# A second pair of solve tiles, and more dense work per recurrence step, in a two-layer hybrid backbone

## The chip, the cores and the metric

The kernel runs on one NeuronCore of a Trainium2 chip. The metric is the device time of one execution in microseconds (us). Each time given for the kernel is a median over runs; the rows come from one further execution that was profiled.

## What is computed

The reference is a backbone of two layers over 1024 latent tokens (x) and 256 context tokens (c) of width 1024. Cut to what matters here, a layer does this, in float32:

```python
ux = modulate(rmsnorm(h)) @ w_in          # 17 blocks of 128 columns
y_rwkv, y_rwkv_c = rwkv7(ux, uc)          # recurrence, forwards and backwards,
                                          # context first, then the latent tokens
y = concat(y_rwkv, pool(ux), fourier(ux), conv(ux))
h  = h + gt1 * (y @ w_out)
h  = h + gt2 * ((silu(g) * u) @ ffn_w_out)     # g, u = modulate(rmsnorm(h)) @ ffn_w_in
hc = the same for the context                  # in layer 0 only
```

The context tokens never read the latent ones, and after layer 0 only the inputs of the context's recurrence are needed. So the whole output side of the context (projection `w_out`, feed-forward) exists in layer 0 alone.

## The kernel before, in words

**Engines and precision.** Every dense product is made of three TensorE matmuls per 128-row piece of the weights: weights and activations are each split into a rounded high part (ACT, a copy, line 324) and the remainder (a subtraction on DVE or POOL, line 325). A 256 KB piece of weights is 128x512 values: one load issued by SP, one ACT copy, one subtraction, twelve matmuls.

**The order of the work.** The program is written as generators that a hand-made weave (`_Weave`) advances; the framework then assigns tiles and orders each engine's instructions by the position in the program and a simulated timeline, so an engine's order is fixed before the run. Within an engine, and on SP's queue of transfers, instructions start in that order.

**The recurrence** (`rwkv2`, line 800) works in chunks: ten stages per layer, two of the context and eight of x, each holding 128 tokens of both directions. An iteration `it` runs from -3 to 9, has 14 gaps (`GAPS`), and carries several stages at once:

- `prep` of stage it+3, from gap 8 (line 896): decays and scaled keys; ACT, POOL lines 921, 943, 957, 971, DVE lines 926 (a scan), 947 to 956.
- `inner` of stage it+2, from gap 0 into the next iteration (line 973): products of keys masked by DVE (line 991) into W; 32x32 blocks of it go through a DRAM tensor `Ad` (line 995) and come back laid out as 32 small triangular systems per partition group in two tiles `As0`, `As1` (line 1001); POOL sets their diagonals (line 1029); then the **solve** (lines 1031 to 1052), a chain of small DVE operations in eight blocks, four from each tile; its result leaves through `Td` (line 1056) and comes back (line 1062).
- `front_b` of stage it+1 (line 1069): merges the solved halves, and transposes values.
- `chain` of stage it (line 1133): the state itself, two chunks with three or four small matmul groups and ACT copies each.
- `finish` of stage it-1 (line 1192): group norm, bonus and gate; for a context stage its end sets `R.ctx`.

The tiles of the recurrence are rings (`rg`, line 855) cut out of one pool `t2` of 73 tiles of 128x512 values. Counted from the code, the rings, the mask and the four tiles of small weights hold 69 of them at most; `As0` and `As1` are one tile each.

**Dense work in the recurrence.** In each gap `W.fill(cost)` draws that many microseconds of dense work (by the program's own count, 1/2.4 ns per matmul column) from the generator `fill` (line 1324). How much is drawn per gap is `FILL[layer]`, by iteration: up to -2, -1, and from 0 on. In layer 0 the generator gives, in order: the remaining input projections; the Fourier mixer (`four2`); then nothing until the convolution and pooling are through and the context's recurrence is read out (`R.ctx`, set late in iteration 2); the output projection of the context and of both halves of x (`outp`, line 1648); the context's second norm (`norm2c`); and the first feed-forward product of the context for `NC` of its 22 blocks (`ffn1_ctx`, line 1621). What is left when the recurrence ends is drawn in the stage behind it (the share of the output projection that reads the recurrence's own output, residuals, x's second norm), and the rest flushed at its end (line 1497). During the recurrence the subtraction of line 325 is on POOL.

**The feed-forward of x** (`ffn1`, line 1541) runs 22 blocks of seven products each. For blocks from `NC` on, it also computes the context's block with the same weights, on four more groups of matmuls (lines 1577 to 1617) and one more split (line 1533).

Of the kernel before, what the change touches and what calls it, by code (L numbers as in the profile page):

```python
# [22 lines left out]
NFF = 22  # L23
# [20 lines left out]
MODPE = ((2, 1), (3, 0), (4, 1))  # L44
MK = 7
FR = "c2"
FILL = ((2.6, 1.2, 0.9), (2.3, 1.0, 0.9))
LA = 2
NC = 14
ORD = (1, 0)  # L50
OFILL = (1.0, 0.3, 0.8, 1.0)
LOP = (0, 2, 4)
# [40 lines left out]
class _Kernel:  # L93
# [706 lines left out]
    def rwkv2(s, R, fill):  # L800
# [7 lines left out]
        for it in range(-3, N):  # L808
# [9 lines left out]
            for g in range(GAPS):  # L818
# [23 lines left out]
                W.step()  # L842
                W.fill(FILL[R.l][min(max(it + 2, 0), 2)])
            for _ in ch:
# [6 lines left out]
        while W.live:  # L851
            W.step()
            W.fill(FILL[R.l][2])

# [118 lines left out]
    def inner(s, R, F):  # L973
# [21 lines left out]
                    nc.sync.dma_start(Ad[b, d, :, h].rearrange("u j i -> j u i"), W[r0:r0 + 32, :, 32 * b:32 * b + 32])  # L995
            yield

        As = [s.rg(R, f"As{a}", 1) for a in range(2)]
        Adf = Ad.rearrange("b d u h j i -> (b d u h) (j i)")
        for a in range(2):  # L1000
            nc.sync.dma_start(As[a], Adf[:, a * 512:(a + 1) * 512].unsqueeze(0).broadcast_to([4, 32, 512]))
# [254 lines left out]
    def run(s, nlayers):  # L1256
# [43 lines left out]
        for l in range(nlayers):  # L1300
# [23 lines left out]
            def fill():  # L1324
# [10 lines left out]
                if not last:  # L1335
                    yield from norm2c()
                    for f in range(NC):
                        yield from s.ffn1_ctx(l, f, [a[2] for a in acts2], hid[f])

            def norm2c():  # L1340

                for _ in range(2):
                    yield
                s.lab("norm2")
                hc = s.rows(NK, ("c",))
                for k in range(NK):
                    h2[k][2] = hc[k][2]
                    nc.sync.dma_start(hc[k][2], ho[k][:, 1024:1280])
                yield
                r = yield from s.rstd_g([h2[k][2] for k in range(NK)], 256, D, 0, False, "ps", lambda j: s.t2())  # L1350
                for k in range(NK):
                    acts2[k][2] = s.act_row(("c",))[2]
                for _ in s.norm_g(l, 1, h2, 2, acts2, r):
                    if _ % 2:
                        yield
# [145 lines left out]
    def ffn1_weights(s, l, ctx):  # L1501
# [11 lines left out]
        def sp(x):  # L1513
            hi, lo = s.t2(F32R, "f2"), s.t2(F32R, "f2")
            nc.scalar.copy(hi, x)  # L1515
            s.nw += 1
            (nc.gpsimd if s.nw % 7 in LOP else nc.vector).tensor_tensor(lo, x, hi.bitcast(F32), ALU.subtract)  # L1517
            return hi, lo
# [3 lines left out]
        for f in range(NFF):  # L1522
# [9 lines left out]
            yield sp(a12)  # L1532
            if ctx and f >= NC:
                yield sp(a21)
# [6 lines left out]
    def ffn1(s, l, wg, acts, B, bc, hid):  # L1541
# [4 lines left out]
        def take():  # L1546
            while len(q) <= LA:
                w = next(wg, None)
                if w is None:
                    break  # L1550
                q.append(w)
            return q.pop(0)
# [15 lines left out]
        for f in range(NFF):  # L1568
            s.lab("ffn")
            ctx = bc[0] is not None and f >= NC  # L1570
            w = take()
# [320 lines left out]
```

## Time and profile before

| what | us |
|---|---|
| median of 3 runs | 3343.46 (3340.38 to 3346.46) |
| the profiled execution | 3351.38 |
| its span, first to last instruction | 3349.6 |
| PE busy | 3000.7 (90%) |
| DVE, POOL, ACT busy | 2109.8, 1385.8, 1257.5 |
| mean granted TensorE clock | 0.911 |

The span is read by stages. Layer 0's recurrence reaches to 910, the stage behind it to about 1104, its feed-forward's first product to 1541, the second to about 1820; layer 1 repeats the order, with its recurrence ending at 2594. "PE busy" counts time with a matmul in flight, whatever the clock; the granted clock of a stretch is a share of full speed (1.0 is 2.4 GHz, 0.5 is 1.2 GHz), so the two together say how much of a stretch TensorE could still take. The chain of waits follows the execution back from its last instruction, each time to what released it.

### The profile page before, as it was taken

The numbers are of one execution on the slowest core, as the hardware profiler recorded it, in microseconds if no ns is written. First come the engines' busy times: TensorE is split into PE (matmuls) and PEld (weight loads), VectorE is DVE, ScalarE is ACT, GpSimd is POOL, SyncE is SP. The second block draws the span as 40 slices with busy tenths as digits, with TensorE's granted clock in tenths as the row PEclk, the third lists the DMA queues.
The fourth block names the chain that finished last, engine by engine and source line by source line (L and its number), as shares of the span: only waits on it lengthen the run. The fifth ranks groups of instructions, "written<-read, shape, count | busy, mean of one in ns | idle before, by whom it ended". The sixth has DMA issues, their size and how long they took to land.

```text
span 3349.6 us, 52386 instructions
## 1 busy us (share of the span) xinstructions
PE 3000.7 (90%) x18888; PEld 2410.5 (72%) x18888; DVE 2109.8 (63%) x3498; ACT 1257.5 (38%) x2575; POOL 1385.8 (41%) x1484
## 2 busy tenths in 40 slices
PE   6989997877889999999999978988877799999998
PEld 3657765766678888888888766756665588888787
DVE  6679666666374988644545598666665755554535
ACT  4446433443363222223212455333443433333212
POOL 2366224563168554435310064245550454545400
PEclk8989887787899999999999988987787799999999
DMA  7422344465455444337412212345553322224312
GB/s 265 165 92 97 102 117 136 124 174 156 144 190 164 149 132 151 125 98 233 139 35 78 87 53 90 117 134 139 156 159 88 128 92 79 82 89 164 123 39 78
DMA packets 375818, 415.48 MB, mean 124 GB/s; under 512 B 115587, under 2 KB 214916, under 8 KB 375558
## 3 DMA queue, kind: packets, MB, share of 16 engines
q1 hardware_dynamic: 375558, 412.13, 39.4%
q8 instruction: 149, 2.44, 0.3%
q14 instruction: 111, 0.91, 0.1%
HBM read 306.49 MB, written 100.27 MB: 121 GB/s over the span
## 4 chain that ended last, share of the span: by engine, by line
PE 55%; DVE 14%; DMA 9%; issue 3%; SPq 1%; ACT 1%; POOL 1%; DVEq 0%; POOLq 0%; ACTq 0%
PE pc L153 17%; PE ps L153 17%; PE pb L153 14%; PE pf L153 8%; DMA t<-Ad 3%; DVE c L532 2%; DMA Td<-t 1%; DVE t L1050 1%; DVE t L947 1%; DVE t L1043 1%; DVE f L325 1%; DVE t L956 1%; DVE t L1469 1%; DMA t<-ho 1%; DVE t L1493 1%
## 5 line engine op out<-in xcount | busy, mean ns | idle before, releaser
L153 PE MATMUL pc<-t,f 128*128 128x512 f32 (+1 forms) x3108 | 754.4, 392 | 41.3 <-ACT t L427 16.0
L153 PEld LDWEIGHTS pc<-t,f 128*128 128x128 f32 x3108 | 581.6, 195 | 182.9 <-ACT t L427 20.5
L153 PE MATMUL ps<-t,f 128*128 128x512 f32 (+1 forms) x2094 | 517.0, 393 | 18.4 <-ACT t L324 7.7
L153 PE MATMUL pb<-t,f 128*128 128x512 f32 (+1 forms) x2094 | 470.5, 370 | 8.4 <-ACT t L1468 4.9
L153 PEld LDWEIGHTS ps<-t,f 128*128 128x128 f32 x2094 | 390.8, 190 | 99.8 <-ACT t L324 8.2
L153 PEld LDWEIGHTS pb<-t,f 128*128 128x128 f32 x2094 | 370.4, 190 | 78.8 <-ACT t L1468 6.0
L1515 ACT CAST f<-c 128x512 fp32r<-128x512 f32 x316 | 196.0, 621 | 536.7 <-PE ps L153 132.0
L1517 POOL TENSOR_TENSOR f<-c,f 128x512 fp32r<-128x512 f32 x135 | 186.5, 1381 | 426.2 <-ACT f L1515 411.7
L153 PE MATMUL pf<-t,f 128*128 128x512 f32 (+2 forms) x1500 | 314.2, 364 | 14.2 <-DVE t L1044 4.0
L324 ACT CAST f<-m 128x512 fp32r<-128x512 f32 (+1 forms) x236 | 134.7, 576 | 436.3 <-PE pb L153 226.4
L153 PEld LDWEIGHTS pf<-t,f 128*128 128x128 f32 (+1 forms) x1500 | 249.5, 198 | 61.4 <-ACT f L324 4.4
L530 POOL TENSOR_TENSOR c<-c,cp 128x352 f32<-128x352 f32 (+2 forms) x168 | 183.3, 1092 | 145.9 <-ACT c L523 71.3
L1517 DVE TENSOR_TENSOR f<-c,f 128x512 fp32r<-128x512 f32 x181 | 158.6, 878 | 134.8 <-ACT f L1515 134.4
L153 PE MATMUL pf<-c,f 128*128 128x512 f32 (+1 forms) x704 | 200.5, 416 | 30.0 <-DVE t L1684 20.3
L325 POOL TENSOR_TENSOR t<-c,t 128x512 fp32r<-128x512 f32 (+1 forms) x110 | 135.1, 1266 | 173.8 <-PE ps L153 99.5
L153 PE MATMUL ps<-t,t 64*128 64x128 f32 (+2 forms) x1032 | 159.9, 341 | 38.9 <-DVE t L956 23.4
L532 DVE SCALAR_TENSOR_TENSOR c<-c,dv,c 128x352 f32<-128x352 f32 (+2 forms) x238 | 190.5, 829 | 2.0
L153 PEld LDWEIGHTS ps<-t,t 64*128 64x128 f32 (+1 forms) x1032 | 133.6, 231 | 60.4 <-issue 20.4
L153 PEld LDWEIGHTS pc<-t,t 128*64 128x64 f32 (+2 forms) x2484 | 124.6, 161 | 71.8 <-issue 28.6
L153 PE MATMUL pc<-t,t 128*64 128x64 f32 (+3 forms) x2484 | 156.2, 258 | 20.9 <-DMA t<-t 11.8
L153 PEld LDWEIGHTS pf<-c,f 128*128 128x128 f32 x704 | 131.5, 214 | 60.1 <-issue 19.1
L261 DVE SCALAR_TENSOR_TENSOR cp<-m,sc,cp 128x512 f32<-128x512 f32 x140 | 137.5, 1003 | 43.0 <-DMA m<-in_wmod 42.3
(256 smaller groups left out, 4731.3 us busy)
## 6 DMA issues: line engine op xcount, KB each, us to landing
c<-in_ffin SPq DMA_DIRECT2D x176, 256.0 KB
m<-in_wmod SPq DMA_DIRECT2D x116, 256.0 KB
t<-rw SPq DMA_DIRECT2D x232, 128.0 KB
hid<-t SPq DMA_DIRECT2D x88, 256.0 KB
c<-hid SPq DMA_DIRECT2D x88, 256.0 KB
m<-in_ffout SPq DMA_DIRECT2D x80, 256.0 KB
t<-in_wmod SPq DMA_DIRECT2D x76, 256.0 KB
m<-in_win SPq DMA_DIRECT2D x64, 256.0 KB
```

Source lines behind the costliest of these rows:

```text
L153: s.nc.tensor.matmul(o, l, r, start=start, stop=stop)
L261: nc.vector.scalar_tensor_tensor(acc[t], w, sc, acc[t], ALU.mult, ALU.add)
L324: r = s.nc.scalar.copy(hi, src)
L325: (eng or s.lo_eng).tensor_tensor(lo, src, hi.bitcast(F32), ALU.subtract)
L530: nc.gpsimd.tensor_tensor(g, g, t_, ALU.add)
L532: nc.vector.scalar_tensor_tensor(a, w[:, j:j + m], tap(j), a, ALU.mult, ALU.add)
L947: nc.vector.scalar_tensor_tensor(KRv[:, :, p, 0, 1:64], k2[:, :, p, 1:64], -2.0, P2[:, :, p, 0:63], ALU.mult, ALU.mult)
L956: nc.vector.tensor_tensor(BKv[rows, :, :, 1 - h, :], cv(kd)[rows], cv(iP)[rows], ALU.mult)
L1043: nc.vector.tensor_tensor(tv, at(x, o, [0, m], [1, 4], [32, 4]), at(T_, r0, [32, m], [0, 4], [1, 4]), ALU.mult)
L1050: nc.vector.tensor_tensor(tv, at(x, o + 4, [0, m], [1, n], [32, 4]), at(T_, r0, [32, m], [0, n], [1, 4]), ALU.mult)
L1515: nc.scalar.copy(hi, x)
L1517: (nc.gpsimd if s.nw % 7 in LOP else nc.vector).tensor_tensor(lo, x, hi.bitcast(F32), ALU.subtract)
```

## The change

`FILL` of layer 0 draws 1.5 instead of 1.2 per gap in iteration -1, and 1.6 instead of 0.9 from iteration 0 on; layer 1 keeps its values. `NC` becomes 22 (`NFF`), so that all of the context's blocks come from `ffn1_ctx`, and `ffn1` computes none (the condition `f >= NC` of lines 1533 and 1570 never holds). `As0` and `As1` get two tiles each, in both layers.

```diff
-FILL = ((2.6, 1.2, 0.9), (2.3, 1.0, 0.9))
+FILL = ((2.6, 1.5, 1.6), (2.3, 1.0, 0.9))
 LA = 2
-NC = 14
+NC = NFF
...
-        As = [s.rg(R, f"As{a}", 1) for a in range(2)]
+        As = [s.rg(R, f"As{a}", 2) for a in range(2)]
```

## Rows read from the trace of the kernel before

**Rows 1.** The page's head.
```profile
span 3349.6 us, 52386 instructions
```

**Rows 2.** Busy time by stretch: PE, PEld, DVE, ACT, POOL, clock, DMA share, GB/s.
```profile
716.00:764.00 48.00, 39.30 (x381) 29.86 (x381) 31.57 (x64) 20.18 (x55) 31.14 (x46) 0.89 0.68 192
845.00:882.00 37.00, 37.00 (x350) 27.10 (x350) 15.39 (x24) 13.93 (x34) 11.90 (x13) 1.00 0.48 146
627.00:910.00 283.00, 236.05 (x2395) 186.87 (x2393) 165.02 (x358) 110.45 (x285) 125.73 (x187) 0.83 0.54 152
910.00:1064.00 154.00, 132.97 (x990) 117.81 (x991) 90.53 (x108) 85.53 (x158) 104.86 (x74) 0.93 0.53 174
...
1341.00:1541.00 200.00, 200.00 (x1080) 173.73 (x1078) 111.08 (x153) 56.80 (x98) 77.58 (x55) 1.00 0.36 116
...
2482.00:2527.00 45.00, 32.90 (x372) 26.58 (x370) 32.30 (x71) 16.86 (x48) 17.74 (x31) 0.73 0.49 147
...
2594.00:2664.00 70.00, 47.42 (x280) 36.18 (x281) 49.64 (x64) 33.30 (x61) 23.03 (x15) 0.78 0.45 154
```

**Rows 3.** Single lines: count, min/median/max ns, first and last start in us.
```profile
L1684 DVE SCALAR_TENSOR_TENSOR t<-pf,mod,t x24: 471/737/751, 630.1 to 898.8; 128x512 f32<-128x512 f32 x16, 128x256 f32<-128x256 f32 x8
...
L1246 DVE TENSOR_TENSOR t<-t,pb x5: 674/686/690, 606.9 to 909.7; 128x512 f32<-128x512 f32 x5
...
L1638 DVE TENSOR_TENSOR cp<-pf,cp x14: 407/420/425, 958.7 to 1075.2; 128x256 f32<-128x256 f32 x14
...
L1576 ACT COPY t<-pc x4: 579/582/582, 1103.9 to 1282.8; 128x512 f32<-128x512 f32 x4
...
L1576 ACT COPY t<-pc x3: 577/586/586, 1342.2 to 1493.2; 128x512 f32<-128x512 f32 x3
...
L1576 ACT COPY t<-pb x7: 580/581/582, 2684.3 to 3026.6; 128x512 f32<-128x512 f32 x7
```

**Rows 4.** Groups by line, 1030 to 1075: busy us, mean ns, idle before.
```profile
L153 PE MATMUL pf<-t,c 128*128 128x256 f32 x356 | 43.4, 284 | 0.2 <-POOL c L325 0.2
...
L325 POOL TENSOR_TENSOR c<-m,c 128x512 fp32r<-128x512 f32 x26 | 33.0, 1293 | 8.8 <-ACT c L324 8.7
L324 ACT CAST c<-m 128x512 fp32r<-128x512 f32 x25 | 15.4, 619 | 20.6 <-DMA m<-in_ffin 16.4 <-PE pf L153 3.5 <-POOL c L325 0.4
```

**Rows 5.** Who waited at line 1029 (us, times), and the chain of waits, 620 to 760.
```profile
  DMA t<-Ad: 173.3, 33
...
638.18 1.22 DVE t L926
...
665.30 0.69 DVE t L991
...
669.99 10.09 DMA t<-Ad
...
680.13 0.13 POOL t L1029
```

**Rows 6.** Timeline of SP's queue: start, us, line, transfer.
```profile
664.67 2.12 SPq L995 DMA_DIRECT2D Ad<-t  x4
...
668.25 0.57 SPq L1001 DMA_DIRECT2D t<-Ad  x1
...
669.99 4.68 SPq L1001 DMA_DIRECT2D t<-Ad  x1
```

**Rows 7.** Timelines of POOL and DVE, one solve operation twice.
```profile
667.28 1.28 POOL L325 TENSOR_TENSOR f<-m,f 128x512 fp32r<-128x512 f32 x1 [6.21 <-ACT f L324]
...
667.54 1.06 DVE L1052 TENSOR_TENSOR t<-t,g 128x28 f32<-128x28 f32 x1
...
676.99 0.20 DVE L1052 TENSOR_TENSOR t<-t,g 128x28 f32<-128x28 f32 x1
```

**Rows 8.** Timelines of ACT and PE: a late weight.
```profile
680.54 0.62 ACT L324 CAST f<-m 128x512 fp32r<-128x512 f32 x1 [7.31 <-DMA m<-in_wout]
...
681.21 0.80 PE L153 MATMUL pf<-c,f 128*128 128x256 f32 x2 [5.14 <-ACT f L324]
```

## The prediction

> **What bounds the kernel now.** I read the busy table by stretch first, multiplying PE's busy time by the granted clock of its row: that is the work at full speed, and the rest of the stretch is lost to idling or to the half-speed clock. Three kinds of stretch appear [rows 2].
>
> - Layer 0's recurrence, from the first output projection (630) to the last read-out (910) [rows 3]: 283 us, 236.0 busy at 0.83 = 196 us of work, 87 lost. No engine is full; it runs on latencies.
> - The stage behind it, 910 to 1064: 132.97 x 0.93 = 124 of work, 30 lost. All 14 context blocks run here (958.7 to 1075.2) [rows 3]. I end it at 1064 because the third block of x's feed-forward copies at 1103.9, and a block takes (1282.8 - 1103.9) / 9 = 19.9 [rows 3].
> - The feed-forward with the context in it, 1341 to 1541: PE 200.00 of 200.00 at clock 1.00. TensorE is the bound, and only fewer matmuls help.
>
> The chain of waits says what the recurrence's latency is. POOL's diagonal for one solve ends at 638; the next stage's scan starts at once (638.18), its masked products come at 665.30, the load of its triangles at 669.99 takes 10.09, and POOL's next diagonal is at 680.13 [rows 5]: a loop of some 42 us, closed because POOL runs this diagonal ahead of the next stage's `prep`.
>
> **The change part by part.**
>
> *Eight context blocks leave x's feed-forward.* With the context a block takes (1493.2 - 1342.2) / 6 = 25.2, without it 19.9 [rows 3]. Eight times 5.3 is 42 us, on a full TensorE: gone from there.
>
> *They reappear in the dense generator.* A block there has 48 matmuls of 256 columns at 43.4 / 356 = 0.122 us, so 5.85 us [rows 4]; eight are 47 us of PE. Each also brings four loads of 256 KB, four ACT copies (0.62) and four POOL subtractions (1.29) [rows 4]; eight splits of the old path go. That is 32 loads more in all.
>
> *The generator is drawn faster.* From the read-out of the context to the end of iteration 9 there are seven iterations. By the program's own count they drew 7 x 12.6 = 88, of which the output projection takes 82 (20.5 for the context, 30.7 for each half of x): the recurrence ended with the blocks still to do. Now they draw 7 x 22.4 = 157, and the read-out behind them some 19: about 18 of 22 blocks move into the recurrence, the rest stays behind it. Iterations 0 to 2 gain nothing, as the generator gives nothing until `R.ctx`.
>
> *What it costs there.* Total PE work from 627 to the start of x's feed-forward becomes 196 + 124 + 47 = 367. The question is what is lost beside it. For steps with a solve I compare two: 24 us of work in 45 (2482 to 2527) and 35 in 48 (716 to 764) [rows 2]: 11 more work, 3 more time. A step of the new kernel has some 46; on that slope it takes about 51 and loses about 5 or 6. Four such steps lose 24; iterations 7 to 9 and the read-out, with few solves left, I put at 12 together, since 845 to 882 is already full (37.00 of 37.00, clock 1.00) [rows 2]. Bounds: 0 lost, or 87 as now. I take 36, nearer to the full step, because most of the blocks fall into such steps. Behind the recurrence the nearest row is layer 1's same stage, with no dense work left: 70 us, 47.42 x 0.78 = 37 work, 33 lost [rows 2]; three or four blocks fill some: 26.
>
> So 367 + 36 + 26 = 429 instead of 437 (627 to 1064), 8 less, and with the 42 about 50 us.
>
> *Queues.* Eighteen moved blocks put 18 x 5 transfers on SP at up to 0.57 us each [rows 6], 51 us over some 330; SP's issues have room, but a load that waits for a free buffer holds up the triangles behind it. ACT (110 of 283 busy) and DVE (165) [rows 2] have room. POOL takes 18 x 4 x 1.29 = 93 us more on 126 [rows 2, 4]; the loss of 5 or 6 per step stands for this queueing, and the second rival prices it in full.
>
> *The second pair of tiles.* It removes a wait of the triangles' load for the solve before. On SP the products are written at 664.67, the first load goes at 668.25, the second, which waits for the solve, at 669.99 [rows 6]: 1.7 us later, 1.1 more than the 0.57 of an issue. The load is late because its data are. So about 1 us per step: 6 in layer 1, 3 in layer 0 before the dense steps take over, 9 in all. From above: POOL's waits for these loads sum to 173 us over both layers [rows 5], some 85 per layer; if the scheduler moved them off the loop, layer 1 would gain up to 70. From below: two of the four tiles that the pool had free are gone, and a reordered POOL could block longer: 20 us lost.
>
> **A rule against it.** One solve operation of 28 elements takes 1.06 us beside a POOL subtraction of 1.28 and 0.20 alone [rows 7], so 0.86 of delay can ride on each moved subtraction. The Trainium skill ("SBUF — State Buffer", "SBUF: two separate sides") says why: GpSimd and a VectorE operation with two SBUF inputs exclude each other for the whole instruction. By that rule, with every moved subtraction hitting the solve, the sum would lose 18 x 4 x 0.86 = 62 more and the gain would be gone. I take it as part of the 36, since most blocks come when the last solve is done; the slower rival uses the delay.
>
> **The sum.** 50 + 9 = 59 off the profiled 3351.4 (a span of 3349.6 [rows 1] and 1.8 around it) is 3292. The median of the runs stands 7.9 below the profile, so I forecast 3285. A measurement can tell about 0.2%, 6.7 us.
>
> **The rivals.**
>
> 1. *Forecast:* dense work fills the idling, TensorE nearly full; 3250 to 3315. Chance 0.56.
> 2. *The triangles' load leaves the loop as well.* The scheduler, free of the old wait, puts POOL's diagonal elsewhere, and layer 1 gains its 70. For it: 173 us of waits [rows 5]. Against: the products come 4 us before the load is issued, so there is nothing to load earlier. 3285 - 64 = 3221. Chance 0.13.
> 3. *Slower: POOL, in the loop, becomes the bound.* Between one diagonal and the next load stand `prep`'s POOL operations, and weight subtractions between them. The context's projection puts 8 more into its step (10 us), x's projection 2.5 blocks more per step (a full and a half subtraction each, 1.94: 4.8, three times), the first step with context blocks 18 of 1.29 less the 6 us there now (16): 41 us on the loop if none hides. A late weight stops PE as well (5.14 us behind a copy that waited 7.31 [rows 8]), and the chain behind it in PE's order. Then the recurrence loses 87 + 41 = 128, not 36: 3285 + 92 = 3377. It decides against the change once the loss passes 95, that is, once the dense work adds to the steps in full and the idling stays. Against: the slope of 3 us for 11. Chance 0.18.
> 4. *The blocks don't fit in.* The context's norm needs 12 tiles of a pool with 2 to 4 free until `prep` of the last stage is through in iteration 6 or 7. If all 22 blocks then run behind the recurrence, 47 are added there and 42 taken from x's feed-forward; with the 9, 3340. Chance 0.13.
>
> **How the numbers follow.** Faster by over 0.2%: 0.56 + 0.13 and a little of case 4, 0.71; within: 0.11; slower: 0.18. The range takes in case 2 and case 4 and leaves out case 3 and a stronger case 2: 3217 to 3350. The forecast's own is 3250 to 3315.
>
> **What would show it.** Right: the context's blocks mostly between 770 and 960; the recurrence's read-out later, near 960 instead of 910, with clock above 0.9; the stage behind it some 75 us; every block of x's feed-forward at 19.9; layer 1's recurrence unchanged within 10 us. Wrong: context blocks still behind the read-out (case 4); layer 1's loop well below 42 us (case 2); the read-out past 1020, POOL full and PE's clock no higher (case 3).

## The result and the profile after

The changed kernel takes 3370.38 us (median of 4 runs, 3362.7 to 3373.65) beside 3341.92 for the kernel before on the same chip (4 runs, 3336.74 to 3346.46): 1.0082 times, 95% interval 1.0059 to 1.0105, 28 us slower where 57 faster was forecast. Its profiled execution is the fastest of its four (3362.70), and that of before stood above its median, so the two profiles differ by 11 us only; stage by stage they are compared as they are.

Single lines of the kernel after, as in [rows 3] (count, min/median/max ns, first and last start in us):

```profile
L1684 DVE SCALAR_TENSOR_TENSOR t<-pf,mod,t x24: 467/742/751, 656.2 to 882.1; 128x512 f32<-128x512 f32 x16, 128x256 f32<-128x256 f32 x8
...
L1246 DVE TENSOR_TENSOR t<-t,pb x5: 672/676/687, 621.3 to 971.9; 128x512 f32<-128x512 f32 x5
...
L1638 DVE TENSOR_TENSOR cp<-pf,cp x8: 423/424/426, 908.0 to 965.8; 128x256 f32<-128x256 f32 x8
...
L1638 DVE TENSOR_TENSOR cp<-pf,cp x22: 409/423/426, 908.0 to 1119.9; 128x256 f32<-128x256 f32 x22
...
L1576 ACT COPY t<-pb x8: 579/581/589, 1081.9 to 1523.2; 128x512 f32<-128x512 f32 x8
...
L1612 DVE TENSOR_TENSOR t<-t,t x22: 675/871/1716, 1096.5 to 1540.4; 128x512 f32<-128x512 f32 x22
```

The last of these rows (line 1612 follows the last of x's seven products in each block) in the kernel before:

```profile
L1612 DVE TENSOR_TENSOR t<-t,t x22: 677/694/1074, 1032.1 to 1540.4; 128x512 f32<-128x512 f32 x22
```

The output projection begins 26 us later than before (656.2 against 630.1 [rows 3]), the recurrence is read out 62 later (971.9 against 909.7), and 8 of the 22 context blocks are done by then (the third row), 14 behind it. x's feed-forward starts its last block at 1523.2; before, that row read 1519.0, but there the last block still had the context in it, some 5 us more to do: line 1612 starts for the last time at 1540.4 in both. So layer 0 has gained nothing: all that its feed-forward saved had been spent.

Busy time by stretch, kernel after (columns as in [rows 2]): the recurrence from the begin of the output projection to the read-out, the stage behind, the feed-forward, and layer 1's recurrence.

```profile
656.00:972.00 316.00, 268.56 (x2806) 216.77 (x2807) 180.89 (x362) 140.85 (x336) 174.42 (x214) 0.91 0.59 165
972.00:1107.00 135.00, 121.47 (x851) 107.90 (x849) 86.01 (x94) 76.35 (x136) 94.39 (x66) 0.92 0.54 181
1186.00:1506.00 320.00, 320.00 (x1464) 266.62 (x1463) 252.59 (x328) 97.00 (x163) 163.80 (x114) 1.00 0.44 142
2084.00:2614.00 530.00, 426.63 (x3801) 323.60 (x3800) 335.58 (x735) 199.50 (x507) 207.69 (x360) 0.79 0.46 126
```

Two of these for the kernel before, on its own marks:

```profile
630.00:910.00 280.00, 233.05 (x2363) 184.27 (x2362) 165.02 (x358) 109.69 (x283) 123.91 (x184) 0.83 0.54 153
...
2085.00:2594.00 509.00, 419.78 (x3797) 314.84 (x3795) 328.68 (x736) 198.32 (x506) 208.09 (x359) 0.82 0.47 131
```

Work is busy time times clock again. From the output projection's begin to the read-out it is 268.56 x 0.91 = 244 us in 316, where before it was 233.05 x 0.83 = 193 in 280: 51 more work cost 36 more time. In the feed-forward TensorE is full (320.00 of 320.00 at clock 1.00), and every block takes the 20 us of one without the context. Layer 1, where the second pair is the only edit, takes 530 us from its first scan to its last read-out instead of 509.

POOL's wait at line 1029 for the triangles, which the second pair was to shorten, grew from 173.3 us [rows 5]:

```profile
  DMA t<-Ad: 222.1, 35
```

With the pair alone it is 185.3, with the faster draw of iterations -1 to 2 alone 190.7.

### The profile page after: what moved, and what is told of

Read it like the earlier page. It is cut to its first block, busy times and chain, and to the rows that moved or that the text cites. A ratio compares the mean times of both kernels' runs of the same rounds, so it can differ in the third digit from the quotient of the medians.

```text
span 3360.9 us, 52525 instructions
## 1 busy us (share of the span) xinstructions
PE 2989.7 (89%) x18888; PEld 2400.5 (71%) x18888; DVE 2127.6 (63%) x3487; ACT 1277.9 (38%) x2605; POOL 1440.3 (43%) x1519
## 4 chain that ended last, share of the span: by engine, by line
PE 58%; DVE 20%; DMA 11%; issue 4%; POOL 3%; SPq 2%; ACT 2%; DVEq 0%; POOLq 0%; ACTq 0%
PE ps L153 17%; PE pc L153 17%; PE pb L153 14%; PE pf L153 10%; DVE c L532 4%; DMA t<-Ad 3%; DVE t L1050 1%; DMA Td<-t 1%; DVE t L1043 1%; DVE t L956 1%; DMA t<-in_wmod 1%; DVE t L1493 1%; DVE t L1052 1%; DVE t L947 1%; DVE t L401 1%
## 5 line engine op out<-in xcount | busy, mean ns | idle before, releaser
L1517 POOL TENSOR_TENSOR f<-c,f 128x512 fp32r<-128x512 f32 x132 | 179.7, 1361 | 418.8 <-ACT f L1515 397.7
L153 PE MATMUL pf<-t,f 128*128 128x512 f32 (+2 forms) x1116 | 260.7, 389 | 15.8 <-DMA f<-eo 4.7
L153 PEld LDWEIGHTS pf<-t,f 128*128 128x128 f32 (+1 forms) x1116 | 199.2, 199 | 60.9 <-ACT t L427 5.2
L153 PEld LDWEIGHTS pc<-t,t 128*64 128x64 f32 (+2 forms) x2484 | 117.7, 153 | 68.0 <-issue 38.6
L153 PE MATMUL pc<-t,t 128*64 128x64 f32 (+3 forms) x2484 | 147.5, 250 | 18.6 <-DMA t<-t 13.7
```

What stands on the lines that cost most here:

```text
L153: s.nc.tensor.matmul(o, l, r, start=start, stop=stop)
```

## The experiments

Each was run beside the kernel before, in five groups of runs (medians of the kernel before 3339.62 to 3344.7); a ratio is to the kernel before of its own group. The marks are of each profiled execution: first output projection (line 1684), last read-out of layer 0 (1246), start of the last block of x's feed-forward (1576), and layer 1 from first scan (926) to last read-out.

| kernel | median us | ratio [95%] | projection | read-out | last block | layer 1 |
|---|---|---|---|---|---|---|
| before | 3341.9 | 1 | 630 | 910 | 1519 | 509 |
| after | 3370.4 | 1.0082 [1.0059, 1.0105] | 656 | 972 | 1523 | 530 |
| pair_only | 3366.6 | 1.0074 [1.0050, 1.0098] | 635 | 915 | 1526 | 526 |
| fill_blocks | 3355.8 | 1.0035 [1.0019, 1.0051] | 666 | 981 | 1532 | 515 |
| fill_only | 3351.6 | 1.0028 [1.0009, 1.0047] | 662 | 976 | 1527 | 512 |
| blocks_only | 3352.2 | 1.0028 [1.0011, 1.0045] | 633 | 913 | 1534 | 513 |
| early | 3367.7 | 1.0078 [1.0058, 1.0098] | 661 | 931 | 1540 | 513 |
| late | 3334.8 | 0.9980 [0.9962, 0.9997] | 631 | 956 | 1506 | 513 |
| later | 3347.9 | 1.0022 [1.0004, 1.0039] | 631 | 967 | 1517 | 523 |
| pool72 | 3364.3 | 1.0065 [1.0052, 1.0078] | 633 | 917 | 1528 | 529 |
| ttlate | 3376.2 | 1.0108 [1.0087, 1.0130] | 647 | 921 | 1533 | 536 |
| pair_ttlate | 3351.1 | 1.0031 [1.0018, 1.0044] | 628 | 907 | 1517 | 526 |
| head | 3357.9 | 1.0049 [1.0032, 1.0065] | 630 | 911 | 1519 | 523 |
| late_head | 3344.3 | 1.0007 [0.9995, 1.0020] | 635 | 956 | 1506 | 523 |
| g | 3377.5 | 1.0121 [1.0093, 1.0149] | 649 | 918 | 1531 | 535 |
| early_g | 3385.9 | 1.0131 [1.0114, 1.0148] | 653 | 926 | 1537 | 528 |
| two | 3354.5 | 1.0047 [1.0031, 1.0062] | 630 | 907 | 1521 | 526 |
| two_pair | 3374.2 | 1.0108 [1.0086, 1.0130] | 636 | 920 | 1529 | 526 |
| two_late | 3337.4 | 0.9994 [0.9980, 1.0007] | 630 | 953 | 1500 | 523 |
| two_early | 3381.0 | 1.0116 [1.0099, 1.0133] | 659 | 937 | 1550 | 523 |

How far a mark can be trusted is seen where nothing was reordered. `blocks_only` runs POOL, DVE and ACT in layer 0's recurrence, instruction by instruction, in the order of before, and its marks there are 3 later; `fill_only` and `late` do so in layer 1's, and it is 2 and 3 longer. `later` and `fill_blocks` have almost the same order in layer 1 and differ by 7. So a difference of up to some 7 us in one mark can be chance of the one execution. The last block's start also flatters the kernels with `NC` at 14: from there on they have some 5 us more to do.

### The parts alone

The pair alone (`pair_only`), the two other edits together (`fill_blocks`), and each of these alone (`fill_only`, `blocks_only`):

```diff
-        As = [s.rg(R, f"As{a}", 1) for a in range(2)]
+        As = [s.rg(R, f"As{a}", 2) for a in range(2)]
```


> The second pair of solve tiles alone, FILL and NC as before. Theory A (the pair is what costs: it leaves two tiles fewer in the pool of 73 and lets the scheduler put the transfers of one solve's result ahead of the next solve's data on SP's queue): layer 1's last read-out ends near 2614 instead of 2594 as in the changed kernel, layer 0's recurrence is longer too, by 10 to 25 us; 20 to 45 us slower than before. Theory B (the pair is harmless in layer 0, the dense work alone stretches its steps): layer 1 still about 20 later, layer 0's read-out within 5 us of 910; 15 to 22 us slower.

```diff
-FILL = ((2.6, 1.2, 0.9), (2.3, 1.0, 0.9))
+FILL = ((2.6, 1.5, 1.6), (2.3, 1.0, 0.9))
-NC = 14
+NC = NFF
```


> FILL and NC changed, one pair of solve tiles. Layer 1 as before in both theories (read-out 2594 less whatever layer 0 gains). Theory A: layer 0's iteration 2 goes back from 61 us to about 40 and the feed-forward ends 20 to 40 us before 1541; 3300 to 3322. Theory B: layer 0 nets to nothing, as in the changed kernel, where its feed-forward ends at 1540 against 1541; 3335 to 3348.

The `FILL` line alone, `NC` at 14:

> FILL changed, NC 14 and one pair. The 14 blocks can be drawn in the recurrence, the other eight stay in x's feed-forward at 25.2 us a block. Theory A: the stage behind the recurrence shortens by more than the recurrence grows, 10 to 25 us faster. Theory B: the recurrence grows by what the stage behind it loses; within 7 us of before.

`NC = NFF` alone:

> NC 22 alone. The drawn amount per step is as before, so the eight blocks land behind the recurrence: 8 x 5.85 = 47 us there, 42 off x's feed-forward. Both theories: 0 to 10 us slower than before; a gain would say that the stage behind the recurrence has idle PE time of its own that these blocks use.

The pair alone costs 22 us (3366.56 against 3344.70), 17 of them in layer 1; the other two edits together cost 11. The sum of 33 agrees with the 28 of the whole change, as each figure's interval is 5 to 8 us to either side. Of those two, the blocks alone cost 7.5: they run behind the recurrence, so 47 us of work is added there and 42 saved, as the rival "the blocks don't fit in" priced it. Drawing faster alone costs 7 and leaves the read-out at 976, as late as with `NC` at 22 (981). It too has 8 blocks done by then, in a recurrence whose POOL, DVE and ACT run in the same order: it is the pace of the draws, not how many blocks the generator holds, that stretches the recurrence.

### When the faster draw begins

Two kernels, `early` and `late`, have a fourth value of `FILL` from iteration 3 on (`+ (it > 2)` in the index of line 843). `early` raises only the draws of iterations -1 to 2, with `NC` at 14; in those iterations hardly any of the moved work exists.

```diff
+FILL = ((2.6, 1.5, 1.6, 0.9), (2.3, 1.0, 0.9, 0.9))
```


> One pair, NC 14, FILL 1.5 and 1.6 only in iterations -1 to 2, 0.9 from iteration 3 on: the early raise alone, with no context block moved into the recurrence. Theory C: the recurrence grows by 20 to 30 us and nothing pays for it; 3362 to 3375. Theory D: the Fourier mixer is drawn an iteration sooner and that is all; within 8 us of before, 3337 to 3353.

`late` raises only the others, with `NC = NFF`:

```diff
+FILL = ((2.6, 1.2, 0.9, 1.6), (2.3, 1.0, 0.9, 0.9))
```


> One pair, NC 22, FILL as before up to iteration 2 and 1.6 per gap from iteration 3 on, where the generator first has something to give after its pause. Theory C (the raised draw in iterations -1 and 0 alters the order of POOL: the chain's decay product of line 1158 and the scan's input come to stand behind the diagonal of line 1029, which waits for its load; 30 of the 68 us by which the recurrence grew are lost there, before any block moves): layer 0's iteration 3 begins near 631 instead of 661, the read-out ends 940 to 955, the whole 3320 to 3335. Theory D (the dense work adds in full wherever it stands): 3348 to 3358, as FILL and NC with the early raise.

The early raise alone costs 27.5 us and moves no context block. The late one, with all 22 blocks out of x's feed-forward, is the one kernel of the study whose interval lies below 1: 0.9980 [0.9962, 0.9997], 5 us faster. Its rows (single lines, then the stretch from the projection to the read-out):

```profile
L1684 DVE SCALAR_TENSOR_TENSOR t<-pf,mod,t x24: 470/740/751, 630.6 to 864.2; 128x512 f32<-128x512 f32 x16, 128x256 f32<-128x256 f32 x8
...
L1638 DVE TENSOR_TENSOR cp<-pf,cp x8: 413/424/427, 889.5 to 950.3; 128x256 f32<-128x256 f32 x8
...
L1576 ACT COPY t<-pb x8: 579/582/584, 1064.4 to 1506.5; 128x512 f32<-128x512 f32 x8
```
```profile
630.00:956.00 326.00, 274.11 (x2880) 223.61 (x2879) 185.43 (x375) 148.06 (x352) 182.89 (x232) 0.90 0.58 166
```

The projection begins where it did before (630.6), and the last block starts 12.5 us earlier than in the kernel before (with the 5 us that the last block itself saves, 17). But the stretch to the read-out has 274.11 x 0.90 = 247 us of work and is 46 longer than before, for 54 more work: each moved microsecond costs 0.85. Still only 8 blocks fit.

Why the early raise costs so much is seen in the order of POOL's instructions, which is fixed in the program. S is line 921 for stage S, D the two diagonals of line 1029, g line 1158 (two for each stage of `chain`), dg line 971; the same stretch of four kernels:

```
before     S3 dg3 g2 dg3 g3 D3a S4 D3b dg4 g4 D4a D4b g5 S5 dg5 g6 g7 D5a D5b S6
late       S3 dg3 g2 dg3 g3 D3a S4 D3b dg4 g4 D4a D4b g5 S5 dg5 g6 g7 D5a D5b S6
early      S3 dg3 g2 D3a D3b g3 S4 dg4 g4 dg4 D4a D4b g5 S5 dg5 S6 g6 dg6 D5a D5b g7
after      S3 dg3 g2 D3a D3b g3 S4 dg4 g4 dg4 D4a D4b g5 S5 dg5 S6 g6 D5a D5b dg6 g7
```

The faster draw puts S4 and g3 behind both diagonals of stage 3 and S6 ahead of g6; `late` keeps the order of before. What that does is seen in the timeline of the kernel after (start, us, engine and line; in brackets the idle time before and what ended it):

```profile
554.10 0.13 POOL L1029 MEMSET t<- 128x16 f32 x1 [13.96 <-DMA t<-Ad]
558.47 0.13 POOL L1029 MEMSET t<- 128x16 f32 x1 [4.24 <-DMA t<-Ad]
560.20 1.30 POOL L1158 TENSOR_TENSOR gg<-t,pcs 64x256 f32<-64x256 f32 x2
561.55 1.22 PE L153 MATMUL pc<-gg,cv 128*128 128x256 f32 x2 [16.67 <-POOL gg L1158]
562.30 1.20 POOL L921 TENSOR_SCALAR t<-t 128x512 f32<-128x512 f32 x2
...
599.18 0.13 POOL L1029 MEMSET t<- 128x16 f32 x1 [12.47 <-DMA t<-Ad]
...
603.64 1.30 POOL L1158 TENSOR_TENSOR gg<-t,pcs 64x256 f32<-64x256 f32 x2
604.99 1.22 PE L153 MATMUL pc<-gg,cv 128*128 128x256 f32 x2 [12.50 <-POOL gg L1158]
...
633.88 1.21 POOL L921 TENSOR_SCALAR t<-t 128x512 f32<-128x512 f32 x2 [15.05 <-ACT t L917]
635.05 2.22 POOL L1158 TENSOR_TENSOR gg<-t,pcs 64x256 f32<-64x256 f32 x2
```

and of the kernel before, the same instructions:

```profile
554.91 0.13 POOL L1029 MEMSET t<- 128x16 f32 x1 [5.78 <-DMA t<-Ad]
554.99 1.21 POOL L921 TENSOR_SCALAR t<-t 128x512 f32<-128x512 f32 x2
557.83 0.13 POOL L1029 MEMSET t<- 128x16 f32 x1 [1.63 <-DMA t<-Ad]
...
588.48 0.13 POOL L1029 MEMSET t<- 128x16 f32 x1 [15.27 <-DMA t<-Ad]
...
596.18 1.30 POOL L1158 TENSOR_TENSOR gg<-t,pcs 64x256 f32<-64x256 f32 x2
597.53 0.70 PE L153 MATMUL pc<-gg,cv 128*128 128x256 f32 x2 [1.90 <-POOL gg L1158]
...
611.64 1.29 POOL L1158 TENSOR_TENSOR gg<-t,pcs 64x256 f32<-64x256 f32 x2
```

D3a comes at the same time in both (554.10, 554.91). In the kernel after POOL then stands 4.24 us before D3b, and behind it wait g3, which PE has waited 16.67 for, and S4, the input of the next stage's scan: 562.30 instead of 554.99, 7 late. The next triangles are 11 late (D4a at 599.18 instead of 588.48), and g5, behind D4 in both kernels, makes PE wait 12.50 instead of 1.90. Then S6, now ahead of g6, waits 15.05 for ACT, and g6 comes at 635.05 instead of 611.64. From 510 to the projection TensorE has the same work in both (before, then after):

```profile
510.00:630.00 120.00, 91.47 (x1034) 71.18 (x1030) 77.74 (x180) 53.93 (x148) 57.48 (x105) 0.70 0.47 128
```
```profile
510.00:656.00 146.00, 99.87 (x1072) 81.11 (x1072) 83.83 (x195) 56.22 (x153) 66.93 (x127) 0.63 0.43 113
```

91.47 x 0.70 = 64 us of work in 120, and 99.87 x 0.63 = 63 in 146. So the 26 us are not work that was added; as I read the timelines, the two latency chains of the recurrence, scan to solve and state to state, hold each other up on POOL. How the 26 us split among these places, and how much of them the lower clock of the emptier stretch costs, was not measured.

### Is it that wait of POOL?

First the diagonals and the small operations of lines 1029 to 1035 of the second tile put on DVE, where the first tile's solve already runs, so that POOL never waits for the triangles:

```diff
-            e, x = (nc.vector, nc.gpsimd)[a], As[a][:, :]
+            e, x = nc.vector, As[a][:, :]
...
-            s.pin(nc.gpsimd.memset(at(x, 16 * a, [33, 16]), 1.0))
+            s.pin(nc.vector.memset(at(x, 16 * a, [33, 16]), 1.0))
```


> The kernel before with the head of both halves of the solve (lines 1029 to 1035) on DVE: POOL never waits for the triangles' load. Theory H (POOL's wait in program order closes the loop from one load to the next): steps of 42 us lose 2 to 8 us each, 18 of them; 3240 to 3315. Theory I (DVE takes over the wait and holds up what POOL held up): 3330 to 3360.

The same with `late`:

> The late raise of FILL with NC 22 and one pair, and the solve's head on DVE. Theory H: faster than the late raise alone (3334.8) by 20 to 90 us. Theory I: 3325 to 3355.

Then line 1158 on DVE, so that the chain's product cannot stand behind POOL's wait; with `early`, and alone as its control:

```diff
-                    nc.gpsimd.tensor_tensor(dpn(Sd[own[h]]), ...
+                    nc.vector.tensor_tensor(dpn(Sd[own[h]]), ...
```


> The early raise alone (as in the run that was 27 us slower), with the chain's decay product of line 1158 on DVE instead of POOL, so that it can't stand behind POOL's diagonal and its wait for the load. Theory C1 (that product behind the wait is what the early raise costs): 3340 to 3352, layer 0's read-out back from 931 to 905 to 918. Theory C2 (the loss comes from the rest of the new order: scan input, stores and loads on SP): 3358 to 3372.

> The kernel before with line 1158 on DVE: the control that the early raise with that move lacked (it was 46 us slower than before). Theory C1 (the early raise costs through that product behind POOL's wait; moving it costs something of its own): this control alone is 30 us or more slower, 3368 to 3385, layer 0's read-out at 920 to 930, so that the early raise adds less than 15 us to it. Theory C2 (the early raise costs elsewhere): 3335 to 3358, read-out at 905 to 915, so that the raise still adds 28 or more.

Taking POOL's wait away gains nothing: `head` costs 18 and `late_head` 4 (9 or 10 more than `late`). In `head` POOL no longer waits there, and DVE idles 155.8 us ahead of line 1031, before 125.5; yet layer 0 is as before (911, 1519). So POOL's wait by itself is not what sets the recurrence's length there. Layer 1 is 14 longer; why it alone is not shown, as the solves lie on one engine in both layers.

Moving the product costs 36 us by itself, so `early_g` gained nothing over `early`. Beside its control it tells more. Without the move, the early raise puts the projection back by 31.3 us (630.1 to 661.4) and costs 27.5; with it, 4.1 (649.0 to 653.1) and 9 (45.6 less 36.3, each over the kernel before of its own group). So most of the early raise's price goes away when the chain's product is not in POOL's order, which speaks for the reading of the timelines. As the move makes those iterations slower on its own account (649 instead of 630), some of that may be cover and not cure.

### A dearer step, or the solves?

If it were the steps with a solve that stretch, the faster draw should be cheap after the last solve. `later` takes 1.2 from iteration 3 and 2.2 from iteration 7:

```diff
+FILL = ((2.6, 1.2, 0.9, 1.2, 2.2), (2.3, 1.0, 0.9, 0.9, 0.9))
 NC = NFF
```


> NC 22, one pair, layer 0 drawing 1.2 per gap from iteration 3 and 2.2 from iteration 7 on: most of the moved blocks fall into the two iterations and the read-out that carry no solve. If it is the steps with a solve that dense work stretches, the read-out ends at 935 to 955 with as many blocks done, and the whole is 8 to 25 us faster than before, 3315 to 3332; if dense work adds in full wherever it stands, no better than the raise from iteration 3 on: 3333 to 3345.

It did not turn cheap: `later` is 7 us slower than before and 12 slower than `late`. Its stretch from the projection to the read-out:

```profile
631.00:967.00 336.00, 301.45 (x2926) 250.00 (x2925) 182.74 (x374) 149.20 (x355) 186.88 (x234) 0.85 0.56 163
```

301.45 x 0.85 = 256 of work in 336: 63 more than before, 56 us longer. The last operation of a solve ends at 836 before and at 860 here; divided there, before:

```profile
630.00:836.00 206.00, 164.06 (x1761) 133.74 (x1760) 134.67 (x310) 79.97 (x214) 107.85 (x168) 0.80 0.57 160
836.00:910.00 74.00, 68.98 (x602) 50.53 (x602) 30.35 (x49) 29.72 (x70) 16.06 (x16) 0.92 0.44 132
```

and in `later`:

```profile
631.00:860.00 229.00, 195.00 (x1825) 155.31 (x1825) 142.65 (x313) 90.21 (x234) 123.44 (x184) 0.78 0.55 158
860.00:967.00 107.00, 106.46 (x1108) 94.69 (x1105) 40.09 (x61) 58.99 (x122) 63.44 (x50) 1.00 0.57 174
```

Beside the solves, 21 more work (152 for 131) took 23 us; behind the last solve, 43 more (106 for 63) took 33. There TensorE itself is the bound: with 63 us of full-speed work in 74 it had 11 left before, and now it is full (106.46 of 107 at clock 1.00).

### Why the second pair costs

One theory was the pool: two more tiles of `t2` for the pair are two fewer for the rest. Against the kernel before with one tile less:

```diff
-T2 = 73
+T2 = 72
```


> The kernel before with 72 tiles in the pool instead of 73: half of what the second pair takes away, and nothing else changed in the program. Theory F1 (the pair's 22 us are a shortage of tiles): 7 to 15 us slower, layer 1's recurrence 516 us or more from first scan to last read-out. Theory F2 (they come from the new order of the queues and engines): within 5 us of before, 505 to 514.

One tile less costs 24, as much as the pair, and in the same place (529 in layer 1). But the pair with two tiles given back does not come free. `two` frees them (the ring `Tt` of the solve's result 1 deep, the gate's half tile in a buffer of its own), `two_pair` spends them on the pair:

```diff
-        Tt = s.rg(R, "Tt", 2)
+        Tt = s.rg(R, "Tt", 1)
...
-        gl = s.rg(R, "gg", 1)[:, 0:256].rearrange("q (d t) -> q d t", d=2)
+        gl = s.big.tile([128, 256], F32, tag="gl", name=s.nm("gl_"), bufs=1).rearrange("q (d t) -> q d t", d=2)
```


> The kernel before with two tiles of the pool set free: the solve's result ring Tt one deep, and the gate's half tile in a buffer of its own. Theory F1 (the pool is short, and each tile counts about as in the run with 72): 5 to 20 us faster, unless 73 is just enough, then within 5. Against it: Tt one deep makes a solve wait for the store of the one before; 5 to 15 slower.

> The same two tiles set free and given to the second pair, so that as many stay free as in the kernel before. Theory F1 (the pair costs by its tiles alone): within 6 us of the run with two tiles free and no pair, layer 1's recurrence 505 to 515. Theory F2 (it costs by the order that it brings): 12 us or more slower than that run, 520 or more.

Freeing them costs 15 by itself, the worst that was expected of it. `two_pair` is 20 us above `two` (3374.18 and 3354.54), though as many tiles stay free in it as in the kernel before. The profiles don't show where: that of `two` took 14 us more than its median, that of `two_pair` 8 less, and in layer 1 both read 526. So the shortage is not the whole cause. What it does in layer 1 stays open, as `two` has two tiles more, no pair, and 526 as well. The two other draws with the tiles of `two`:

> The late raise of FILL with NC 22, one pair, and two tiles set free. Theory F1: faster than the late raise alone (6 us under the kernel before) by as much as the two tiles give there; 3315 to 3335. Otherwise 3330 to 3345.

> The early raise alone (28 us slower) with two tiles set free. If its loss is a shortage of tiles as well (the Fourier mixer's three tiles meeting the rings while they fill), it falls to 0 to 12 us over the run with two tiles free; if it is the fixed order of the engines in the steps without dense work, it stays at 18 to 30 over it.

`two_early` is 26 above `two`, as `early` is 27.5 above before, with the projection at 659: the early raise is not a matter of tiles either. `two_late` is no faster than `late`.

The other theory was SP's queue. Its timeline (start, us, line, transfer) for one stage in layer 1, before:

```profile
2304.59 1.80 SPq L995 DMA_DIRECT2D Ad<-t  x4
...
2307.14 1.98 SPq L995 DMA_DIRECT2D Ad<-t  x4
...
2310.28 0.57 SPq L1001 DMA_DIRECT2D t<-Ad  x1
...
2311.67 0.56 SPq L1001 DMA_DIRECT2D t<-Ad  x1
2312.28 0.54 SPq L1056 DMA_DIRECT2D Td<-t  x1
...
2322.58 1.80 SPq L1062 DMA_DIRECT2D t<-Td  x4
```

and the same stage in `pair_only`:

```profile
2313.11 2.62 SPq L995 DMA_DIRECT2D Ad<-t  x4
2315.82 0.57 SPq L1056 DMA_DIRECT2D Td<-t  x1
2316.49 2.21 SPq L302 DMA_DIRECT2D m<-in_wout  x1
2318.79 1.22 SPq L876 DMA_DIRECT2D t<-rw  x2
2320.64 1.29 SPq L1062 DMA_DIRECT2D t<-Td  x3
2322.04 2.42 SPq L995 DMA_DIRECT2D Ad<-t  x4
...
2325.86 1.16 SPq L1001 DMA_DIRECT2D t<-Ad  x2
```

DVE has masked the second products of this stage by 2316.70:

```profile
2315.41 1.29 DVE L991 TENSOR_TENSOR t<-ps,cv 128x512 f32<-128x512 f32 x2 [0.34 <-PE ps L153]
```

With one pair the triangles' second load goes 1.4 us after the first (2310.28, 2311.67), 0.8 more than an issue takes. With two it goes at once. But the store of the solve before now stands ahead of the second products' store, and so does the load of its result, which starts 4.8 us after it: the second products leave at 2322.04, 5.3 us after they were ready, and the triangles' loads 12.8 us after the first products began, instead of 5.7 and 7.1. In those 5.3 us SP also issues a weight and two other reads; it stands idle for 0.6 only. To test whether this costs, that load (line 1062) was put three gaps later, with the pair (`pair_ttlate`) and, as control, without (`ttlate`):

```diff
+        for _ in range(3):
+            yield
+        s.lab(f"rsolve.{F.seg}{F.i}")
         F.TT = s.rg(R, "TT", 3)
```


> The second pair alone, and the loads of the solve's result (line 1062) three gaps later, so that on SP they no longer stand ahead of the next stage's products while they wait for their own store. Theory E (the pair costs through SP's order): layer 1's recurrence, from its first scan to its last read-out, goes back from 526 us to 505 to 514, the whole to 3340 to 3352. Theory F (it costs through the two tiles it takes from the pool, or through POOL's order): still 520 or more, the whole 3358 to 3370.

> The later loads alone, one pair, FILL and NC as before: the control of the run before it. Theory E: the kernel before has the same hold-up in about half of its steps, so 0 to 15 us faster, 3330 to 3345. Theory F: no change, 3340 to 3350.

With the pair this recovers half (11 instead of 22), all of it before layer 1, whose recurrence stays at 526. Without the pair the same edit costs 36. So the theory fell for layer 1. One thing the runs say together: no kernel that edits the pool, a queue or an engine in layer 1 keeps its 509 us (523 to 536), while those that edit layer 0's draws or blocks alone have 512 to 515, `later` (523) excepted. Not every new order costs. `blocks_only` and `early` change layer 0 alone, yet layer 1 follows in another order than before, the same in both, and takes 513; `later` and `fill_blocks` share a third (523 and 515). So the orders that the pair brings (526 to 530) are bad ones, but which displaced instruction costs the 17 is not settled; nor does POOL's wait at line 1029 measure it, for it is 134.5 us in `two`, which is slower than before.

## Why the prediction was wrong

**The saving, right.** Eight blocks leave x's feed-forward and each of its blocks takes 19.9 instead of 25.2: from 1107, the mark that answers to 1064 (the fifth and sixth blocks start 44 us later than before), the feed-forward needs 416 to the start of its last block, against 455: 39 less for the seven of the eight blocks that lie before that mark, where the forecast had 37 for seven and 42 for eight.

**Where the forecast lost.** It had 429 us from 627 to that mark; the changed kernel takes 480 (to 1107). With the pair's 9 less in the forecast and 21 more in layer 1, these 51 and 30 are 81 of the 85 us between 3285 and 3370.

**"Iterations 0 to 2 gain nothing": the step that failed most.** They were costed at nothing because the generator gives nothing there. It gives the input projections and the Fourier mixer before that, and the faster draw brings those forward. `early` shows 27.5 us for this raise alone, the projection 31 late; in the changed kernel it is 26 late. Beside the later raise it costs the whole less: `fill_blocks` is 11.1 above before and `late` 5.4 below, 16.5 apart, each figure with an interval of 5 to 6 us to either side. The timelines show where: POOL's order, in which scan inputs and the chain's products came to stand behind other waits. I had looked at queues for the moved blocks, not for what a new pace does to the order of the recurrence's own instructions.

**Eighteen blocks into the recurrence: eight.** The sum took 7 x 22.4 = 157 us of draws. But where `outp` and `norm2c` pause (eight pauses in each of three `outp` calls, line 1665 on, and some ten in the norm), `W.fill` drops what the gap was owed, so 34 of the 98 gaps draw nothing. That is read from the code, after the fact, but its sum fits: 157 - 34 x 1.6 + 19 - 82 = 40 us, which by the program's count (5.12 a block) are 7.8 blocks, and 8 were done, the first at 908 instead of 770. All of them lie behind the last solve, which ends at 875.3: what stretched the steps with a solve was the output projection, drawn faster, and not the blocks. The stage behind the recurrence kept 14 blocks and takes 135 us instead of the 75 forecast; its loss (135 - 121.47 x 0.92 = 23) is near the 26 that I had put.

**The loss in the recurrence: 36 forecast, 72 measured**, from the projection to the read-out (316 - 244), 87 before. The slope of 3 us for 11 came from two different steps, one of layer 1 and one of layer 0. Within layer 0, the same stretch at two paces gives 36 for 51 in the changed kernel, 46 for 54 in `late`, 56 for 63 in `later`: 0.7 to 0.9. The idle time in its gaps was not free room.

**The rule on moved subtractions, hardly put to the test.** By the rule weighed in the prediction, every moved subtraction could lengthen a solve operation by 0.86 us, 62 in all. But the subtractions of the context blocks (`c<-m`) begin in the recurrence when the last operation of a solve (line 1044) is over, so that they could meet none:

```profile
L325 POOL TENSOR_TENSOR c<-m,c x40: 1263/1291/1738, 890.2 to 971.8; 128x512 fp32r<-128x512 f32 x40
```
```profile
L1044 DVE TENSOR_REDUCE t<-t x40: 169/228/286, 660.0 to 875.0; 128x4 f32<-128x16 f32 x5, 128x8 f32<-128x32 f32 x5, 128x12 f32<-128x48 f32 x5, 128x16 f32<-128x64 f32 x5
```

From the projection to the read-out line 1052, the operation of [rows 7], took 12.82 us in 35 times before and 13.31 after, and all 210 DVE operations of the solves (lines 1031 to 1052) 75.4 and 83.0. The port that the Trainium skill ("SBUF — State Buffer", "SBUF: two separate sides") describes may cost 0.86 where the two meet [rows 7]; what a block drawn beside a solve would pay, no run here shows.

**The second pair: -9 forecast, +22 measured.** The bound from below, 20 lost to the missing tiles and a reordered POOL, was the right one, and the 1.1 us per step that it removes were real where the load did wait; they came with a worse order of the engines and of SP, and which part of it costs is open.

**The rivals.** Slower came true by a mechanism near the third rival's in one point only: dense work adds to the steps almost in full. Its other half, POOL's subtractions as the bound, did not show: POOL is busy 174 of 316. The fourth came true in part (14 of 22 blocks behind). The second fell: layer 1's loop grew.

In the sum up to the feed-forward: +26 (early raise), +36 (316 for 280), -19 (135 for 154 behind the read-out), -39 (feed-forward): +4 at the start of its last block, as the rows at 1523.2 and 1519.0 show, and nothing at its end (1540.4 in both); then the pair's +21 in layer 1. The two profiles differ by 11 only, as the last stage, 2594 to the end before and 2614 to the end after, is 9 shorter in the second (755.6 and 746.9), with nothing edited there: such is the spread of single executions.

## What to carry to other kernels

Where each engine runs in an order fixed beforehand, an edit of pace or of buffers is also an edit of that order: list what comes to stand behind each long wait before pricing anything at zero, and test each part alone, for here a saving of some 40 us was real and three side effects ate it. Price dense work that is put into a latency-bound loop at most of its own length unless the same loop has been measured at two paces, and read its idle time part by part: behind the last solve TensorE had 11 us left of 74. And count what a generator really gives: a pause in it can drop the share of a gap.

## What was not expected

Edits that only move instructions, with the amount of work unchanged, moved the whole by 7 to 36 us: the 76 operations of 64x256 of one line put from POOL (median 612 ns) to DVE (422 ns) cost 36, a load put three gaps later costs 36, a pool of 72 tiles instead of 73 costs 24. Before and after differ by 28, so effects of order are as large here as any saving under study. The runs of one kernel also spread further than the shown three suggested: `late` has 3319.88 to 3353.03.
